# Norm columns transposed into the next group's accumulator, and x loaded by itself one block ahead

## The chip, the cores and the metric

The kernel runs on one core of one Trainium2 chip. The metric is device time in microseconds (us), the median of the runs. The kernel before took 2122.87 us (median of 3 runs, 2119.78 to 2123.72).

Five engines work side by side, each with its own queue in program order: PE (TensorE, matrix products and transposes), DVE (VectorE), ACT (ScalarE), POOL (GpSimd) and SP (SyncE, which here only issues DMA transfers; ACT can issue them too). An instruction that waits for another engine holds up all that is queued behind it on its own.

## The reference

One layer over two sequences, the prompt (s = 0, 1024 tokens) and the sample (s = 1, 2048 tokens), model width 1024. The input is modulated and projected; half of the width goes through a windowed attention, the other half through a differential attention with 4 heads of two softmaxes each; the results are gated, projected and normalised with the input.

```python
def diff_attention(...):          # per block of 128 queries, 4 heads, 2 maps
    logits = jnp.einsum('bqhmd,bkhmd->bhmqk', qb, kh) * (HEAD_DIM ** -0.5)
    p = jax.nn.softmax(logits + bias[None, :, None], axis=-1)
    w = p[:, :, 0] - lam * p[:, :, 1]
    o = jnp.einsum('bhqk,bkhe->bqhe', w, vh)
    ...
    o = rms_norm(o, subln_w) * (1.0 - lambda_init)

def hybrid_layer(x, c, ...):
    u = x * (1.0 + scale[:, None]) + shift[:, None]
    qa, ka, va, ga, qb, kb, vb, gb = jnp.split(u @ w_in, SPLIT_OFFSETS, axis=-1)
    oa = window_gqa(qa, ka, va, sink, rel_bias) * jax.nn.silu(ga)
    ob = diff_attention(qb, kb, vb, ...) * jax.nn.silu(gb)
    h = jnp.concatenate([oa, ob], axis=-1) @ w_out
    return layer_norm(ALPHA * x + gate[:, None] * h, ln_g, ln_b)
```

The part that the change touches is the factor of `rms_norm`, one number per query and head, and the loading of x for the last line.

## The kernel before

Up to about 1144 us the projections and the windowed attention run. Then comes the differential attention, unit by unit (128 queries of one head), 64 units of the sample sequence and after them 16 of the prompt. Two units of the sample, or one unit of the prompt holding two blocks, form a group of 256 queries. `slot(n, ...)` does unit n in four steps; in a step PE has, in this order, the logits of unit n (L826, into a tile `lg`), the values of earlier groups (L882 to L884, into the group's accumulator, the left half of the PSUM tile `ac` that the code calls `G["O"]`), and four transposes of a unit three slots back (L864, into a tile `tp`, of which there are two). DVE adds the bias and takes the minimum (L831), ACT takes the exponential (L839, 2048 wide for the sample, 1024 for the prompt), DVE and POOL combine the two maps (L841, L844, L848, L850), ACT and DVE split each transposed tile into a high and a low part (L866, L867; L867 is the last reader of `tp`).

When a group's values are done, ACT copies them out (`osb`, L887) and they are stored (L888; by SP, in the last slots by ACT). In the second step of a later slot `square_sum` follows: PE transposes `osb` into the right half of the same accumulator tile (L897, twice), ACT squares each of the two transposes in place and sums it (L899, twice), ACT and DVE form the argument (L901, L903), and POOL takes the power -1/2 (L909) into two columns of a tile `four`. Two groups fill its four columns, so there are 48 sums and 24 stores. `store` turns the four columns into rows: a transpose on PE (L915), a copy on ACT (L917), a DMA on SP (L918) into `frow`.

The order on PE is written out by hand through all slots. The order on the other engines is set by the compiler's scheduler up to unit 79; from slot 80 on (the transition, about 1807 to 1848 us) all engines follow the code, and `outputs()` is stepped in between: it loads and splits the output weights and begins with the output. `load_rest(t)` loads the parts of output block t, `gate_parts(t)` and `join(t)` (POOL and ACT, L1046 to L1057) combine them, `output` multiplies (L1081 to L1083), adds gate and x (L1086, L1087) and normalises; L1123 stores the block. There are 24 blocks of 128 tokens, `load_rest` runs three blocks ahead and `join` two.

Of the kernel before, what the change touches and what calls it, by code (L numbers as in the profile page):

```python
# [11 lines left out]
F32 = mybir.dt.float32  # L12
# [8 lines left out]
P = 128  # L21
# [46 lines left out]
def hybrid_layer(ctx, tc, x_prompt, x_sample, c_prompt, c_sample, w_in, w_out, w_ada, b_ada, ln_g, ln_b,  # L68
                 attn_sink, lambda_q1, lambda_k1, lambda_q2, lambda_k2, subln_w, rel_bias, oh, eye,
                 y_prompt, y_sample):  # L70
    nc = tc.nc
    xs = (x_prompt, x_sample)
# [14 lines left out]
    def tp():  # L87
        return ps_tp.tile([P, 512], F32, tag="tp", name="tp")
# [59 lines left out]
    def load_x(tb, d):  # L148
        s, t0 = (0, tb * CH) if tb < 2 else (1, (tb - 2) * CH)
        xt = x_p.tile([P, 4, P], F32, tag="x", name="x")  # L150
        nc.sync.dma_start(out=xt, in_=xs[s][t0:t0 + CH, d * P:(d + 1) * P].rearrange("(j p) d -> p j d", p=P))
        return xt
# [235 lines left out]
    def fill(n):  # L388
        for _ in range(n):
            next(steps, None)  # L390
# [110 lines left out]
    with tc.issue_after(wload[6]):  # L501
# [15 lines left out]
        for i in range(2):  # L517
            bg = sm2.tile([1, D], F32, tag="bg", name="bg")
            nc.sync.dma_start(out=bg, in_=b_ada[2 * D:3 * D].rearrange("(o d) -> o d", o=1))
            for q in range(2):  # L520
                cs = slice(q * 512, (q + 1) * 512)
# [218 lines left out]
    order = [(s, h) for s in (1, 0) for h in range(HB)]  # L740
# [45 lines left out]
    def prefetch(n, j):  # L786

        s, h, i, g = units[n]
        if j == 1:
            for u in units[n + 1:n + (3 if n >= EARLY - 1 else 2)]:  # L790
                if u[3] == asked[0] + 1 and (u[0] == 0 or u[3] == units[n + 1][3]):
                    load_queries(u[3])
        if n in staged and j == 2:
            stage(staged[n])
        if i == (4 if s else 2) and j == 2 and (s, h) != units[-1][:2]:
            load_head(*next_head[s, h])
        if n + 1 < N and units[n + 1][2] == 0 and j == 3:
            load_keys(*units[n + 1][:2], range(2, SEQS[units[n + 1][0]] // CH))
# [72 lines left out]
    def values(g, piece):  # L871
        s, h, i = groups_of[g]
        T = SEQS[s] // P
        G = groups_[g]
        Vt = heads[s, h][2]
        if piece == 0:
            G["O"] = ac()
        a = G["O"][:, :QG]
        for kb in range(piece * 2, piece * 2 + 2):
            kq, c = divmod(kb, 4)  # L880
            H, L = G["PT"][kq]
            nc.tensor.matmul(a, lhsT=Vt[kq][:, 0, c, :], rhs=H[:, c, :], start=(kb == 0), stop=False)  # L882
            nc.tensor.matmul(a, lhsT=Vt[kq][:, 0, c, :], rhs=L[:, c, :], start=False, stop=False)  # L883
            nc.tensor.matmul(a, lhsT=Vt[kq][:, 1, c, :], rhs=H[:, c, :], start=False, stop=(kb == T - 1))  # L884
        if piece == T // 2 - 1:
            osb = e_p.tile([P, QG], F32, tag="osb", name="osb")
            nc.scalar.copy(osb, a)  # L887
            (nc.sync if now[0] < N * 4 else nc.scalar).dma_start(out=OT[s][h][:, i * P:i * P + QG], in_=osb)  # L888
            G["osb"] = osb

    def square_sum(g):
        s, h, i = groups_of[g]
        G = groups_[g]
        ss = st_p.tile([P, 2], F32, tag="ss", name="ss")
        ot = [G["O"][:, QG + b * P:QG + (b + 1) * P] for b in range(2)]
        for b in range(2):
            nc.tensor.transpose(ot[b], G["osb"][:, b * P:(b + 1) * P], ident)  # L897
        for b in range(2):
            nc.scalar.activation(ot[b], ot[b], AF.Square, accum_out=ss[:, b:b + 1])  # L899
        f = st_p.tile([P, 4], F32, tag="f", name="f")  # L900
        nc.scalar.activation(f[:, 0:2], G["s0"], AF.Square, scale=EPS ** 0.5)  # L901
        for b in range(2):
            nc.vector.tensor_scalar(out=f[:, 2 + b:3 + b], in0=ss[:, b:b + 1], scalar1=1.0 / P,  # L903
                                    scalar2=f[:, b:b + 1], op0=ALU.mult, op1=ALU.add)
        c = i % 4
        if c == 0:
            four[0] = four_p.tile([P, 4], F32, name="four")
        F = four[0]
        nc.gpsimd.tensor_tensor(out=F[:, c:c + 2], in0=f[:, 2:4], in1=mhalf, op=ALU.pow)  # L909
        del groups_[g]  # L910

        def store():

            pf = tp()
            nc.tensor.transpose(pf[0:4, 0:P], F, ident)  # L915
            fr = f_p.tile([4, P], F32, name="fr")
            nc.scalar.copy(fr, pf[0:4, 0:P])  # L917
            nc.sync.dma_start(out=frow[s][h, (i - 2) * P:(i + 2) * P].rearrange("(b p) -> b p", p=P), in_=fr)  # L918

        if c:  # L920
            stores.append((now[0] + 6, store))

    now, stores, four = [0], [], [None]

    def slot(n, extra, other=None):
        for j in range(4):
            now[0] = n * 4 + j
            if extra:
                fill(extra)
            if n < N:  # L930
                logits(n, j)
                prefetch(n, j)
            for g, piece in values_at.get(n, ()):
                if piece % 4 == j:
                    values(g, piece)
            if 0 <= n - LAG < N:
                transpose(n - LAG, j)
            if j == 1 and n in sums_at:
                square_sum(sums_at[n])
            if stores and stores[0][0] <= now[0]:  # L940
                stores.pop(0)[1]()
            if other is not None:
                next(other, None)

# [56 lines left out]
    xts = Views(lambda: value() if len(xts.made) < 3 else part(), 6)  # L1001
# [28 lines left out]
    def load_rest(t):  # L1030

        s, i = order[t]
        cs = slice(i * P, (i + 1) * P)
        d = dat.next().rearrange("p (n i q) -> p n i q", n=4, i=4)
        nc.sync.dma_start(out=d[:, 1], in_=OT[s][:, :, cs].rearrange("k r t -> r k t"))
        nc.sync.dma_start(out=d[:, 2], in_=frow[s][:, cs].partition_broadcast(P))
        nc.sync.dma_start(out=d[:, 3], in_=GB[s][:, :, cs].rearrange("k r t -> r k t"))
        nc.sync.dma_start(out=d[:, 0], in_=OA[s][:, :, cs].rearrange("i r t -> r i t"))
        xt = xts.next().bitcast(F32)
        nc.sync.dma_start(out=xt, in_=xs[s][cs, :])  # L1040
        Bs[t] = dict(s=s, i=i, d=d, xt=xt)

    def gate_parts(t):

        d = Bs[t]["d"]
        nc.gpsimd.tensor_tensor(out=d[:, 1], in0=d[:, 1], in1=d[:, 2], op=ALU.mult)  # L1046
        nc.gpsimd.tensor_tensor(out=d[:, 1], in0=d[:, 1], in1=d[:, 3], op=ALU.mult)

    def join(t):

        B = Bs[t]
        d = B["d"]
        B["oH"], B["oL"] = [v.rearrange("p (k q) -> p k q", k=KC) for v in os_.next()]
        for half in range(2):
            hs = slice(half * 4, half * 4 + 4)
            nc.scalar.copy(B["oH"][:, hs, :], d[:, half])
            nc.gpsimd.tensor_tensor(out=B["oL"][:, hs, :], in0=d[:, half], in1=B["oH"][:, hs, :].bitcast(F32),  # L1057
                                    op=ALU.subtract)
# [66 lines left out]
    order = [(s, i) for s in (1, 0) for i in range(SEQS[s] // P)]  # L1125
    NB = len(order)
    Bs = {}

    def outputs():

        todo = {0: lambda: load_rest(0), 4: lambda: load_rest(1), 6: lambda: load_gate(1), 8: load_norm,
                5: lambda: gate_parts(0), 11: lambda: join(0), 14: lambda: load_rest(2)}
        halves = [(k, n) for k in range(4) for n in range(2)] + [(k, n) for n in range(2) for k in range(4, KC)]
        blocks = out_steps()
        for step in itertools.count():
            if step in todo:
                todo[step]()
            if halves:
                split_weights(*halves.pop(0))
            if step >= 12 and next(blocks, 0) == 0:  # L1140
                return
            yield

    def out_steps():
        for t in range(NB):
            if t == 8:
                load_gate(0)
            for j, _ in enumerate(output(Bs[t], t == NB - 1)):
                if j == 2 and t + 3 < NB:
                    load_rest(t + 3)  # L1150
                if j == 4 and t == 0:
                    gate_parts(1)
                    join(1)
                if j == 12 and t + 2 < NB:
                    gate_parts(t + 2)
                    join(t + 2)
                yield
            del Bs[t]
            yield
# [7 lines left out]
    with tc.manual_schedule(engines=ENGINES):  # L1167
        for n in range(N, max(sums_at) + 1):
            slot(n, 0, other)
        for _ in range(8):  # L1170
            next(other)
        for _, store in stores:
            store()
        for _ in other:
            pass
    st.close()
# [26 lines left out]
```

## Time and profile before

| | us |
|---|---|
| median of 3 runs | 2122.87 |
| profiled execution | 2118.73 |
| its span, first to last instruction | 2116.9 |
| PE busy | 2059.4 (97%) |
| POOL / DVE / ACT busy | 1151.1 / 1300.3 / 1045.9 |
| differential attention, sample | about 1144 to 1660 |
| the same, prompt | about 1660 to 1807 |
| transition | about 1807 to 1848 |
| output blocks | about 1848 to 2108.8 |

The span is the time between the first and the last instruction of one execution; 1.8 us of that execution lie outside it. A busy share is an average over stages, so the stages are read one by one. The trace names each instruction by its line in the code, the tile it writes and the tiles it reads.

### The profile page before, as it was taken

The page shows a single profiled execution, that of the slowest core. Times are in us where ns is not written, and L with a number is a line of the kernel's source. Part 1 is how long each engine was busy: PE and PEld are TensorE (multiplying, and loading weights), DVE is VectorE, ACT ScalarE, POOL GpSimd, SP SyncE. Part 2 cuts the span into 40 slices and gives each one's busy share as a digit, 9 for nine tenths or more (in the row PEclk, how much of TensorE's full clock was granted, in tenths as well). Part 3 has the DMA queues.
Part 4 walks back from the last instruction along what each step waited for, and adds up shares of the span by engine and source line. Part 5 has one row for each costly group of instructions (what it writes and reads, how often), then busy time and mean ns, then how long its engine had stood idle before and what let it go on. Part 6 is the DMA issues. An engine that isn't in the chain of part 4 may idle for free.

```text
span 2116.9 us, 32562 instructions
## 1 busy us (share of the span) xinstructions
PE 2059.4 (97%) x11621; PEld 1769.6 (84%) x11621; DVE 1300.3 (61%) x2536; ACT 1045.9 (49%) x2046; POOL 1151.1 (54%) x830
## 2 busy tenths in 40 slices
PE   7999999999999999999999999999999999799998
PEld 4777898888988888888897888888888899788887
DVE  5335124222225777777654998989898999655555
ACT  5211113111015767777623777777777899622221
POOL 3213213212124344334353888888888899677774
PEclk9999999999999999999999999999999999999999
DMA  9685735435538868778454122122131353557763
GB/s 273 181 292 156 188 120 174 132 122 135 155 115 226 205 167 216 207 194 212 131 164 145 46 83 79 44 91 71 58 102 38 92 169 106 166 146 203 199 196 103
DMA packets 327337, 312.44 MB, mean 148 GB/s; under 512 B 19126, under 2 KB 284086, under 8 KB 326792
## 3 DMA queue, kind: packets, MB, share of 16 engines
q1 hardware_dynamic: 326456, 309.72, 51.4%
q8 instruction: 92, 1.51, 0.3%
q10 hardware_dynamic: 720, 0.66, 0.1%
q14 instruction: 69, 0.57, 0.1%
HBM read 212.70 MB, written 97.60 MB: 147 GB/s over the span
## 4 chain that ended last, share of the span: by engine, by line
PE 87%; DMA 5%; DVE 4%; ACT 1%; POOL 1%; issue 1%; SPq 1%; ACTq 0%; DVEq 0%; POOLq 0%
PE lg L826 14%; PE pj L187 12%; PE pj L188 12%; PE pj L189 12%; PE tp L864 6%; PE po L1083 4%; PE po L1082 4%; PE po L1081 4%; PE ac L882 3%; PE ac L884 3%; PE ac L883 3%; PE lgA L608 3%; PE tp L644 3%; PE ac L636 2%; PE ac L635 1%; DVE l L831 1%
## 5 line engine op out<-in xcount | busy, mean ns | idle before, releaser
L187 PE MATMUL pj<-uH,wH 128*128 128x512 f32 x1040 | 418.0, 402 | 3.4 <-DVE gg L258 3.4
L189 PE MATMUL pj<-uH,wL 128*128 128x512 f32 x1040 | 406.8, 391 | 0.0
L218 POOL TENSOR_TENSOR wL<-wr,wH 128x1024 fp32r<-128x1024 f32 x74 | 181.8, 2459 | 413.5 <-DVE wH L216 373.2
L188 PE MATMUL pj<-uL,wH 128*128 128x512 f32 x1040 | 406.4, 391 | 0.0
L850 POOL TENSOR_TENSOR l<-l,l 128x1024 f32<-128x1024 f32 x160 | 382.8, 2415 | 1.2
L826 PE MATMUL lg<-kt,Q 128*128 128x512 f32 x1280 | 374.8, 414 | 2.1 <-DVE gg L258 1.4
L839 ACT ACTIVATE l<-l,nm 128x2048 f32<-128x2048 f32 (+1 forms) x192 | 330.9, 1724 | 15.8 <-DVE nm L831 15.8
L831 DVE CUSTOM_DVE_ANT_0 l<-lg,W 128x1024 f32<-128x1024 f32 x192 | 233.5, 1216 | 21.4 <-PE lg L826 21.3
L866 ACT CAST pth<-tp 128x512 fp32r<-128x512 f32 x320 | 186.6, 584 | 119.6 <-PE tp L864 111.5
L826 PEld LDWEIGHTS lg<-kt,Q 128*128 128x128 f32 x1280 | 217.1, 189 | 31.9 <-DVE nm L831 2.0
L848 POOL TENSOR_SCALAR l<-l,s 128x1024 f32<-128x1024 f32 x160 | 179.3, 1134 | 100.2 <-DVE s L844 57.3
L189 PEld LDWEIGHTS pj<-uH,wL 128*128 128x128 f32 x1040 | 195.1, 188 | 42.2
L187 PEld LDWEIGHTS pj<-uH,wH 128*128 128x128 f32 x1040 | 195.5, 188 | 36.9 <-DVE gg L258 4.3
L867 DVE TENSOR_TENSOR ptl<-tp,pth 128x512 fp32r<-128x512 f32 x320 | 210.7, 686 | 17.8 <-ACT pth L866 16.4
L188 PEld LDWEIGHTS pj<-uL,wH 128*128 128x128 f32 x1040 | 195.8, 188 | 30.6
L864 PE MATMUL tp<-ident,l 128*128 128x128 f32 x1280 | 192.0, 272 | 5.8 <-DVE ptl L867 5.8
L623 POOL TENSOR_SCALAR l<-l,rcA 128x384 f32<-128x384 f32 (+1 forms) x144 | 81.0, 581 | 191.0 <-DVE rcA L617 97.3
L882 PE MATMUL ac<-pth,vt 128*128 128x256 f32 x640 | 180.9, 283 | 0.0
L884 PE MATMUL ac<-pth,vt 128*128 128x256 f32 x640 | 180.0, 281 | 0.0
L883 PE MATMUL ac<-ptl,vt 128*128 128x256 f32 x640 | 179.1, 280 | 0.0
L831 DVE CUSTOM_DVE_ANT_0 l<-lg,W,nm 128x1024 f32<-128x1024 f32 x128 | 164.0, 1281 | 20.9 <-PE lg L826 15.7
L864 PEld LDWEIGHTS tp<-ident,l 128*128 128x128 f32 x1280 | 147.9, 140 | 8.2 <-DVE ptl L867 5.0
(210 smaller groups left out, 4025.9 us busy)
## 6 DMA issues: line engine op xcount, KB each, us to landing
wr<-in_w_in SPq DMA_DIRECT2D x39, 1024.0 KB, 5.7
KAt<-ka SPq DMA_DIRECT2D x40, 384.0 KB, 7.1
QAt<-qa SPq DMA_DIRECT2D x24, 512.0 KB, 4.8
kt<-kb SPq DMA_DIRECT2D x24, 512.0 KB, 5.2
Q<-qb SPq DMA_DIRECT2D x48, 256.0 KB, 3.3
Q<-qb SPq DMA_DIRECT2D x96, 128.0 KB, 3.1
vt<-vb SPq DMA_DIRECT2D x48, 256.0 KB, 4.6
wa<-in_w_ada SPq DMA_DIRECT2D x32, 256.0 KB, 6.0
```

Of the source, the lines that this page charges most:

```text
L187: nc.tensor.matmul(acc, lhsT=a(k), rhs=b(k), start=(k == 0), stop=False)
L188: nc.tensor.matmul(acc, lhsT=a(k), rhs=bl(k), start=False, stop=False)
L189: nc.tensor.matmul(acc, lhsT=al(k), rhs=b(k), start=False, stop=(k == KC - 1))
L826: nc.tensor.matmul(L[:, c * CH:(c + 1) * CH], lhsT=G["Q"][:, v, m, b * P:(b + 1) * P], rhs=Kt[kt0 + c][:, m, :], start=(v == 0), stop=(v = ...
L831: nc.vector.tensor_tensor_reduce(out=half, in0=L, in1=W[:, off:off + 1024], scale=1.0, scalar=nm[:, m, 0:1] if s and hf else 3e38, op0=ALU ...
L839: nc.scalar.activation(e, e, AF.Exp, bias=nm[:, m, hf:hf + 1], scale=-1.0, accum_out=sums)
L850: nc.gpsimd.tensor_tensor(out=row[:, cs], in0=row[:, cs], in1=rows[n][1][:, cs], op=ALU.add)
L864: nc.tensor.transpose(pt[:, c * P:(c + 1) * P], rows[n][0][:, (j * 4 + c) * P:(j * 4 + c + 1) * P], ident)
L867: nc.vector.tensor_tensor(out=L[:, :, qs], in0=p3, in1=H[:, :, qs].bitcast(F32), op=ALU.subtract)
L882: nc.tensor.matmul(a, lhsT=Vt[kq][:, 0, c, :], rhs=H[:, c, :], start=(kb == 0), stop=False)
L883: nc.tensor.matmul(a, lhsT=Vt[kq][:, 0, c, :], rhs=L[:, c, :], start=False, stop=False)
L884: nc.tensor.matmul(a, lhsT=Vt[kq][:, 1, c, :], rhs=H[:, c, :], start=False, stop=(kb == T - 1))
```

## The change

`store` no longer takes a `tp` tile of its own six steps after its group's sum. It is kept until the next group's `square_sum` and transposes `four` into that group's accumulator tile, rows 0 to 3 of its left half, whose values have been copied to `osb` by then. The last store of all still takes a `tp` tile. In the output part the load of x is taken out of `load_rest` into `load_x`: x of block 0 at step 10, x of block t+1 at the fourth step of block t; `load_rest(t + 3)` moves from the third step of a block to the seventh, and `load_rest(2)` from step 14 to step 16.

```diff
@@ -909,16 +909,18 @@
         nc.gpsimd.tensor_tensor(out=F[:, c:c + 2], in0=f[:, 2:4], in1=mhalf, op=ALU.pow)
         del groups_[g]
 
-        def store():
-
-            pf = tp()
+        if stores:
+            stores.pop()(G["O"])
+
+        def store(pf):
+
             nc.tensor.transpose(pf[0:4, 0:P], F, ident)
             fr = f_p.tile([4, P], F32, name="fr")
             nc.scalar.copy(fr, pf[0:4, 0:P])
             nc.sync.dma_start(out=frow[s][h, (i - 2) * P:(i + 2) * P].rearrange("(b p) -> b p", p=P), in_=fr)
 
         if c:
-            stores.append((now[0] + 6, store))
+            stores.append(store)
 
     now, stores, four = [0], [], [None]
 
@@ -937,8 +939,6 @@
                 transpose(n - LAG, j)
             if j == 1 and n in sums_at:
                 square_sum(sums_at[n])
-            if stores and stores[0][0] <= now[0]:
-                stores.pop(0)[1]()
             if other is not None:
                 next(other, None)
 
@@ -1036,9 +1036,12 @@
         nc.sync.dma_start(out=d[:, 2], in_=frow[s][:, cs].partition_broadcast(P))
         nc.sync.dma_start(out=d[:, 3], in_=GB[s][:, :, cs].rearrange("k r t -> r k t"))
         nc.sync.dma_start(out=d[:, 0], in_=OA[s][:, :, cs].rearrange("i r t -> r i t"))
-        xt = xts.next().bitcast(F32)
-        nc.sync.dma_start(out=xt, in_=xs[s][cs, :])
-        Bs[t] = dict(s=s, i=i, d=d, xt=xt)
+        Bs[t] = dict(s=s, i=i, d=d)
+
+    def load_x(t):
+        s, i = order[t]
+        xt = Bs[t]["xt"] = xts.next().bitcast(F32)
+        nc.sync.dma_start(out=xt, in_=xs[s][i * P:(i + 1) * P, :])
 
     def gate_parts(t):
 
@@ -1129,7 +1132,7 @@
     def outputs():
 
         todo = {0: lambda: load_rest(0), 4: lambda: load_rest(1), 6: lambda: load_gate(1), 8: load_norm,
-                5: lambda: gate_parts(0), 11: lambda: join(0), 14: lambda: load_rest(2)}
+                5: lambda: gate_parts(0), 11: lambda: join(0), 10: lambda: load_x(0), 16: lambda: load_rest(2)}
         halves = [(k, n) for k in range(4) for n in range(2)] + [(k, n) for n in range(2) for k in range(4, KC)]
         blocks = out_steps()
         for step in itertools.count():
@@ -1146,7 +1149,9 @@
             if t == 8:
                 load_gate(0)
             for j, _ in enumerate(output(Bs[t], t == NB - 1)):
-                if j == 2 and t + 3 < NB:
+                if j == 3 and t + 1 < NB:
+                    load_x(t + 1)
+                if j == 6 and t + 3 < NB:
                     load_rest(t + 3)
                 if j == 4 and t == 0:
                     gate_parts(1)
@@ -1169,8 +1174,7 @@
             slot(n, 0, other)
         for _ in range(8):
             next(other)
-        for _, store in stores:
-            store()
+        stores.pop()(tp())
         for _ in other:
             pass
     st.close()
```

In the changed kernel's line numbers L915, L917 and L918 are L917, L919 and L920, and the load of x is L1044 instead of L1040.

PE in the sample sequence, kernel before, at a step with a store (`four` holds the four norm columns):

```order
L884 MATMUL ac<-pth,vt 128x256
L864 MATMUL tp<-ident,l_13634 128x128 [waits DVE_49]
L864 MATMUL tp<-ident,l_13634 128x128 x3
L915 MATMUL tp<-ident,four 4x128 [waits DVE_49,PE_49,Pool_49]
L826 MATMUL lg<-kt,Q 128x512 x4
L882 MATMUL ac<-pth,vt 128x256 [waits Activation_49]
```

The transpose of the norm columns waits there for DVE and POOL. PE in the changed kernel, at a step with a store:

```order
L864 MATMUL tp<-ident,l_13725 128x128 [waits DVE_49]
L864 MATMUL tp<-ident,l_13725 128x128 x3
L897 MATMUL ac<-ident,osb 128x128 [waits Activation_49]
L897 MATMUL ac<-ident,osb 128x128
L917 MATMUL ac<-ident,four 4x128 [waits Activation_49,Pool_49]
L826 MATMUL lg<-kt,Q 128x512 [waits DVE_49]
L826 MATMUL lg<-kt,Q 128x512 x3
L882 MATMUL ac<-pth,vt 128x256
```

The transpose has moved directly behind the two transposes of the next group's sum, and waits for ACT and POOL. ACT in the sample sequence, kernel before, around a store and the next sum:

```order
L839 ACTIVATE l_13934,s0g<-l_13934,nm 128x2048 [waits DVE_49]
L917 COPY fr<-tp 4x128 [waits DMAHW0_49,PE_49]
L866 CAST pth<-tp 128x4x128 [waits PE_49] x2
L899 ACTIVATE ac,ss<-ac 128x128 [waits PE_49,Activation_49]
L839 ACTIVATE l_13989,s_13988<-l_13989,nm 128x2048 [waits DVE_49,Pool_49]
L899 ACTIVATE ac,ss<-ac 128x128 [waits Activation_49]
```

ACT in the changed kernel at the same place:

```order
L839 ACTIVATE l_13928,s0g<-l_13928,nm 128x2048 [waits DVE_49]
L866 CAST pth<-tp 128x4x128 [waits PE_49] x2
L899 ACTIVATE ac,ss<-ac 128x128 [waits PE_49,Activation_49]
L839 ACTIVATE l_13978,s_13977<-l_13978,nm 128x2048 [waits DVE_49,Pool_49]
L899 ACTIVATE ac,ss<-ac 128x128 [waits Activation_49]
L919 COPY fr<-ac 4x128 [waits DMAHW0_49,PE_49]
```

The copy of the rows has moved behind the second of the next sum's squares; an exponential stands between the two squares, as before. ACT in the transition, kernel before, at the fourth of its five stores of a group (`DMAHW0` to `DMAHW7` are eight semaphores that transfers take in turn; a transfer is issued when the one before it on its semaphore has landed):

```order
L1022 ACTIVATE wo<-kt,wsub 128x512
L887 COPY osb<-ac 128x256 [waits DMAHW1_49,PE_49]
L888 DMA ot_81<-osb 128x256 [waits DMAHW0_49,Activation_49]
L1022 ACTIVATE wo<-kt,wsub 128x512
L1056 CAST pth<-l_19029 128x512 [waits DMAHW6_49]
```

The same place in the changed kernel:

```order
L1022 ACTIVATE wo<-kt,wsub 128x512
L887 COPY osb<-ac 128x256 [waits PE_49]
L888 DMA ot_81<-osb 128x256 [waits DMAHW2_49,Activation_49]
L1022 ACTIVATE wo<-kt,wsub 128x512
L1059 CAST ptl<-l_19006 128x512 [waits DMAHW5_49]
```

The store has another semaphore, because one transfer more or fewer stands ahead of it in the order of issue.

## Rows read from the trace of the kernel before

**Rows 1.** The page's section on the chain that ended last, by engine and line.

```profile
PE 87%; DMA 5%; DVE 4%; ACT 1%; POOL 1%; issue 1%; SPq 1%; ACTq 0%; DVEq 0%; POOLq 0%
```

**Rows 2.** Three stages: length, busy us (instructions) by engine, clock, DMA share, GB/s.

```profile
1144.00:1660.00 516.00, 502.28 (x3371) 455.71 (x3372) 466.75 (x891) 396.57 (x660) 434.01 (x271) 1.00 0.25 76
1660.00:1807.00 147.00, 146.06 (x996) 133.72 (x995) 137.36 (x300) 132.41 (x288) 136.69 (x90) 1.00 0.43 128
1848.00:2108.80 260.80, 260.71 (x1151) 213.19 (x1149) 138.17 (x239) 57.81 (x97) 184.54 (x160) 0.99 0.62 174
```

**Rows 3.** Sixteen steps of the sample sequence, same columns.

```profile
1453.29:1488.14 34.85, 33.92 (x229) 30.93 (x230) 31.39 (x61) 26.77 (x46) 29.18 (x19) 1.00 0.13 39
```

**Rows 4.** PE's waits, 1000 to 1807 us: total us, times, longest.

```profile
PE tp L915 <- DVE ptl L867: 13.1, 14, 0.9
```

**Rows 5.** PE's instructions, a step without and one with a store: start, length.

```profile
1484.53 0.60 PE L864 MATMUL tp<-ident,l 128*128 128x128 f32 x4
1484.89 0.48 PE L826 MATMUL lg<-kt,Q 128*128 128x512 f32 x1
...
1486.62 0.60 PE L864 MATMUL tp<-ident,l 128*128 128x128 f32 x4
1488.14 0.27 PE L915 MATMUL tp<-ident,four 128*4 128x128 f32 x1 [0.93 <-DVE ptl L867]
1488.16 0.94 PE L826 MATMUL lg<-kt,Q 128*128 128x512 f32 x3
```

**Rows 6.** PE at a sum of squares, sample sequence.

```profile
1474.37 0.38 PE L897 MATMUL ac<-ident,osb 128*128 128x128 f32 x2
1474.51 0.94 PE L826 MATMUL lg<-kt,Q 128*128 128x512 f32 x3
```

**Rows 7.** ACT over the same sum.

```profile
1475.05 0.28 ACT L899 ACTIVATE ac<-ac 128x128 f32<-128x128 f32 x1
...
1475.34 2.00 ACT L839 ACTIVATE l<-l,nm 128x2048 f32<-128x2048 f32 x1
...
1477.32 0.27 ACT L899 ACTIVATE ac<-ac 128x128 f32<-128x128 f32 x1
1477.52 0.19 ACT L899 ACTIVATION_READ_ACCUMULATOR ac<-ac 128x1 f32 x1
```

**Rows 8.** PE and ACT at a sum of the prompt sequence.

```profile
1786.01 0.94 PE L826 MATMUL lg<-kt,Q 128*128 128x512 f32 x3
...
1786.84 1.15 ACT L839 ACTIVATE l<-l,nm 128x1024 f32<-128x1024 f32 x1
...
1788.17 0.19 ACT L899 ACTIVATION_READ_ACCUMULATOR ac<-ac 128x1 f32 x1
```

**Rows 9.** ACT and PE in the transition, waits in brackets.

```profile
1823.76 0.59 ACT L866 CAST pth<-tp 128x512 fp32r<-128x512 f32 x1 [4.00 <-DMA ot<-osb]
...
1844.53 0.72 ACT L1022 ACTIVATE wo<-kt,wsub 128x512 fp32r<-128x512 f32 x1 [7.61 <-DMA l<-gb]
...
1846.95 0.36 ACT L887 COPY osb<-ac 128x256 f32<-128x256 f32 x1
...
1825.12 0.66 PE L864 MATMUL tp<-ident,l 128*128 128x128 f32 x4 [2.84 <-DVE ptl L867]
...
1847.36 0.69 PE L897 MATMUL ac<-ident,osb 128*128 128x128 f32 x2 [3.51 <-ACT osb L887]
```

**Rows 10.** PE behind the last of these waits: busy, clock, as in rows 2.

```profile
1848.00:1850.00 2.00, 2.00 (x7) 1.52 (x6) 1.65 (x5) 1.35 (x7) 1.25 (x3) 0.50 0.96 180
1850.00:1852.00 2.00, 2.00 (x9) 1.66 (x8) 0.00 (x0) 0.00 (x0) 1.92 (x3) 0.82 0.85 311
```

**Rows 11.** SP and POOL in the output blocks: two issues, one wait.

```profile
1905.39 0.35 SPq L1123 DMA_DIRECT2D out<-pth  x1
...
1908.87 5.00 SPq L1040 DMA_DIRECT2D vt<-in_x_sample  x1
...
POOL l L1046 <- DMA l<-frow: 18.3, 11, 2.8
```

## The prediction, made before the changed kernel was run

> **What bounds the kernel now.** I read the chain that ended last first: 87% of it is PE [rows 1], so a microsecond counts where PE is held up. The stages then say where PE has time left: it is busy 502.28 of 516.00 us in the sample's differential attention, 146.06 of 147.00 in the prompt's, and 260.71 of 260.80 in the output blocks [rows 2]. Time can be won only in the gaps of the first and in the transition; it can be lost anywhere. Sixteen steps of the sample, with one store in them, take 34.85 us, of which PE works 33.92, DVE 31.39, POOL 29.18 and ACT 26.77 [rows 3]: PE sets the pace, the others have 3.5 to 8.1 us to spare, and the 0.93 us that PE misses is one wait. That wait is at the transpose of the norm columns, L915, for DVE's subtraction L867: 14 times between 1000 and 1807 us, 13.1 us in all [rows 4]. The store takes one of two `tp` tiles, and DVE has not yet read the one it gets.
>
> **What goes at the stores.** In a step without a store the logits L826 start 1484.89 - 1484.53 = 0.36 us behind the first of the four transposes L864; with one, 1488.16 - 1486.62 = 1.54 [rows 5]. The difference, 1.18 us, leaves that step: the 0.93 of wait and what the refilling of PE costs. 14 stores have it; the six other stores before the transition show no such wait and give back nothing I count.
>
> **What comes at the sums.** The transpose now stands directly behind the two L897 of the next group's sum and ahead of the next logits, and the rows of the order give it a wait for ACT and one for POOL. POOL's power is a whole group old by then, so it is free. ACT's is not. The L897 just ahead has already waited for ACT's copy `osb`; a further wait for ACT can only be for something ACT does later, and the only later ACT work on that accumulator tile is the two squares L899, which work in place on the half that the L897 have just written. The rows of ACT in the changed kernel fit: the copy of the new rows stands behind the second square.
>
> So PE would wait for the second square, and between the two squares ACT has an exponential. At 1474 us the first square starts at 1475.05, the exponential takes 2.00, and the reading of the second square's sum ends at 1477.52 + 0.19 = 1477.71 [rows 7]. PE starts 0.05 us after ACT is done where a row shows that pair: copy ended at 1846.95 + 0.36 = 1847.31, L897 at 1847.36 [rows 9]. L826 follows L915 by 0.02 [rows 5]. The logits would start at 1477.78 instead of 1474.51 [rows 6], 3.27 us late. Behind L917 in PE's queue stand the logits, the values and the next transposes, so nothing on PE fills this. DVE's L831 waits for the logits, and the exponentials for DVE; they have the 3.5 us and more of rows 3 to catch up, so I add nothing for them. Net of a sample store: 3.27 - 1.18 = +2.09; 14 of them **+29.3 us**.
>
> Six more stores meet sums while the exponentials are 1024 wide (1.15 us): there the second square is read at 1788.17 + 0.19 = 1788.36, L826 would be at 1788.43 instead of 1786.01, 2.42 us late [rows 8]; six of them **+14.5 us**. (24 stores: 14, these 6, 3 in the transition, and the last one in a `tp` tile as before.)
>
> Bounds of the wait: from below, no new wait at all (a rival, below); from above the same 3.27 and 2.42 with a fall of the clock behind each.
>
> [...]
>
> **The clock.** PE now idles from the end of L897 at 1474.37 + 0.38 = 1474.75 to about 1477.76, 3.0 us. [...] Behind the wait of 2.84 us at 1825.12, four L864 took 0.66 [rows 9], about the 0.60 of rows 5: no fall. 3.0 is nearer to 2.84, so I take 0; the upper end is 14 x 1.7 = 24 us. [...]
>
> **The transition.** ACT issues the stores of the last groups there and hangs twice for a semaphore that an earlier transfer holds: 4.00 and 7.61 us; PE's waits of 2.84 and 3.51 follow [rows 9]. In the changed order one transfer more or less stands ahead, so each store draws another semaphore. The one that hung behind the load of `gb` now follows a short store of the norm rows; its wait and the fall of the clock go, 3.51 + 1.7 = 5.2. Against it stand three new waits for the squares; they lie next to each other there, so each is about 1.0 (an estimate from two squares of 0.27 and 0.19 each in rows 7, with the way there and back), and two of them fall into waits that PE has anyway. I take **-4.1 us**; the ends are -8 (the 2.84 goes too) and +3 (the 3.51 stays, and all three come on top).
>
> **The output blocks.** Removing the x load from the parts and issuing it for itself changes no instruction on PE, DVE or POOL. x for the next block now goes out directly behind a block's store, the parts behind it instead of ahead. SP spends up to 5.00 us on one x load, and POOL already waits 11 times, 18.3 us, for a part (`frow`) [rows 11]. PE is at 100% and the parts are joined two blocks ahead, so I take 0. From below it is 0 as well, since PE has no gap to close. From above: parts 5.00 us later, of which POOL's free time, (260.80 - 184.54) / 24 = 3.2 per block, hides most; 1.8 us, once in two blocks of the 16 of the sample, is +14.
>
> **The sum.** 29.3 + 14.5 - 4.1 = +39.7 us. The profiled execution took 2118.73 (span 2116.9 and 1.8 outside), which gives 2158.4; it was 4.1 below the median of the runs shown, so on that base **2163 us**.
>
> **Rivals.**
> - *The wait isn't for the squares* (the other side: faster). If ACT's wait at L917 ends with the copy `osb`, PE goes straight on, the 13.1 us of rows 4 and the 5.2 of the transition go, and the time is about 2105. It decides where the logits start no more than 0.3 us behind L897. For it: the two halves of the tile don't overlap. Against it: the L897 ahead has that wait already.
> - *The clock falls at each sample wait*: +24, about 2187. For it: 3.51 did it. Against it: 2.84 did not.
> - *The parts come late*: output blocks longer than before, +14, about 2177. For it: POOL's 18.3 us for `frow`. Against it: the same bytes pass in the same time, and an x load stood between two blocks' parts before as well.
> - *The stores' gain is hidden*: DVE's subtraction is late for an L864 instead, and the wait comes back there. That would add at most 14 x 0.93 = 13, about 2176; the L864 of rows 5 wait for nothing, and the order has one tile less in use, so I give it little and count it with the parts.
>
> **Chances.** Forecast 0.64 (its own range 2155 to 2170, by the ends of the transition); clock 0.18; late parts or tiles 0.10; no wait for the squares 0.05; between it and the forecast, within 0.2%, 0.03. A difference of 0.2%, 4 us, is about what can be told from no change. The range 2150 to 2188 leaves out the fast rival and the clock together with late parts. Faster 0.05, same 0.03, slower 0.92.
>
> **What would show it.** In the profile after: a row "L917 waits for ACT's L899" with some 20 to 23 waits, the longest near 3, about 58 us in all (14 x 3.0, 6 x 2.2 and the transition); no wait of L915's kind for L867; the sixteen steps 34.85 + 2.1 = about 36.9 us long at a clock of 1.00 (below it: the clock rival); output blocks still at 11 us each with PE busy throughout; no wait of 3.5 us near 1847 + 43. The prediction is wrong if L826 starts within 0.3 us of L897 at these sums, or if the blocks grow.

## The result and the profile after

The changed kernel takes 2184.64 us (median of 5 runs, 2180.34 to 2188.64) against 2122.87 before (5 runs): 1.0293 of the time before, 95% interval 1.0273 to 1.0313. It is slower by some 62 us. The profiled execution took 2180.34 us, its span is 2178.3, 61.4 longer than before.

The waits of PE through the differential attention and the transition (total us, times, longest), kernel after; these rows stand where [rows 4] stood:

```profile
PE ac L917 <- ACT ac L899: 56.8, 20, 3.2
PE ac L917 <- ACT f L901: 3.7, 3, 1.6
PE po L1084 <- ACT Q L1059: 2.3, 1, 2.3
PE tp L864 <- DVE ptl L867: 1.9, 4, 0.7
```

Twenty waits of the store's transpose for a square, where before there were 14 for DVE's subtraction; these have gone without coming back at L864 (1.9 us). The second row is the three stores in the transition. It names L901, which ACT does right behind the squares, but there too L917 starts 0.14 us after the second square is read (1876.31 + 0.19 = 1876.50, L917 at 1876.64). The third row is the first product of the output, which waits there for its input. PE and ACT at one store of the sample (start, length, instruction, wait in brackets), which answer to [rows 5 to 7]:

```profile
1248.61 0.38 PE L897 MATMUL ac<-ident,osb 128*128 128x128 f32 x2
1252.09 0.27 PE L917 MATMUL ac<-ident,four 128*4 128x128 f32 x1 [3.09 <-ACT ac L899]
1252.11 0.70 PE L826 MATMUL lg<-kt,Q 128*128 128x512 f32 x2
```

```profile
1249.30 0.27 ACT L899 ACTIVATE ac<-ac 128x128 f32<-128x128 f32 x1
...
1249.58 1.99 ACT L839 ACTIVATE l<-l,nm 128x2048 f32<-128x2048 f32 x1
...
1251.57 0.26 ACT L899 ACTIVATE ac<-ac 128x128 f32<-128x128 f32 x1
1251.76 0.18 ACT L899 ACTIVATION_READ_ACCUMULATOR ac<-ac 128x1 f32 x1
1252.39 0.26 ACT L919 COPY fr<-ac 4x128 f32<-4x128 f32 x1 [0.45 <-PE ac L917]
```

The second square is read at 1251.76 + 0.18 = 1251.94, L917 starts 0.15 us later, and the logits 3.50 us behind L897 instead of 0.14. At a store of the prompt the exponential is shorter, and so is the wait:

```profile
1743.15 0.38 PE L897 MATMUL ac<-ident,osb 128*128 128x128 f32 x2
1745.77 0.37 PE L917 MATMUL ac<-ident,four 128*4 128x128 f32 x1 [2.24 <-ACT ac L899]
```

3.09 - 2.24 = 0.85 us, just what the exponentials differ by (2.00 and 1.15, [rows 7, 8]).

Four cycles of sixteen steps with one store each, kernel after, columns as in [rows 3] (the clock stands in front of the last two):

```profile
1215.10:1252.09 36.99, 33.90 (x230) 30.85 (x231) 31.58 (x61) 26.88 (x45) 29.14 (x19) 1.00 0.12 37
1252.09:1289.09 37.00, 33.91 (x230) 30.91 (x230) 31.56 (x61) 26.89 (x45) 27.57 (x19) 0.99 0.37 112
1364.29:1404.01 39.72, 36.63 (x229) 33.24 (x230) 31.66 (x61) 26.88 (x45) 29.09 (x19) 0.92 0.11 34
1517.90:1557.64 39.74, 36.65 (x230) 33.26 (x231) 31.66 (x61) 26.89 (x45) 29.05 (x19) 0.93 0.11 34
```

In the first two PE works 33.9 us as before and waits 3.09 instead of 0.93: 37.0 against 34.85. In the others the same matrix products take 36.6 us. The stretches of 2 us behind the store at 1364.29 show why:

```profile
1364.30:1366.30 2.00, 2.00 (x6) 1.63 (x7) 0.09 (x1) 0.26 (x1) 2.00 (x2) 0.50 0.05 9
1366.30:1368.30 2.00, 2.00 (x12) 2.00 (x10) 1.23 (x2) 0.00 (x0) 1.05 (x2) 0.50 0.00 0
1368.30:1370.30 2.00, 2.00 (x7) 1.61 (x7) 0.74 (x2) 0.59 (x1) 0.00 (x0) 0.51 0.00 0
1370.30:1372.30 2.00, 2.00 (x15) 1.83 (x15) 1.45 (x3) 0.82 (x2) 0.00 (x0) 1.00 0.41 124
```

PE idled 3.09 us, and for the next 6 its clock was granted at 0.50. Behind the equally long wait at 1252.09 it stayed at 1.00:

```profile
1252.10:1254.10 2.00, 2.00 (x14) 1.82 (x15) 0.87 (x2) 0.26 (x1) 2.00 (x2) 1.00 0.02 5
```

Set the first L897 of each sum side by side in the two traces, and the whole loss can be read off as steps of the difference:

```
stretch                         what                             us
sample, 14 stores               steps of +3.34 to +3.36          +46.9
                                further, at 8 of the 14          +13.6
sample, 14 steps of the store   -1.19 to -1.22 each              -16.9
prompt, 6 stores                steps of +2.39                   +14.3
                                further, at 5 of the 6            +7.9
transition and output blocks                                      -3.6
start (other work, ends earlier) and rounding                      -0.8
sum, as between the two spans                                    +61.4
```

The output blocks were as long as before and PE was busy throughout:

```profile
1930.00:2169.70 239.70, 239.70 (x1065) 196.39 (x1064) 127.44 (x218) 53.42 (x84) 169.32 (x145) 1.00 0.66 183
```

POOL's wait for `frow` shrank from 18.3 us [rows 11] to 6.1. From 1912 to 2168 us, kernel after:

```profile
POOL ve L1100 <- DMA l<-frow: 3.8, 2, 1.9
...
POOL l L1049 <- DMA l<-frow: 2.3, 6, 0.6
```

### The profile page after: what moved, and what is told of

It reads as the page before. It is cut to its first block, busy times and chain, and to the rows that moved or that the text cites. A ratio compares the mean times of both kernels' runs of the same rounds, so it can differ in the third digit from the quotient of the medians.

```text
span 2178.3 us, 32604 instructions
## 1 busy us (share of the span) xinstructions
PE 2079.4 (95%) x11621; PEld 1787.4 (82%) x11621; DVE 1306.9 (60%) x2536; ACT 1049.4 (48%) x2046; POOL 1152.4 (53%) x830
## 4 chain that ended last, share of the span: by engine, by line
PE 88%; DMA 4%; issue 2%; ACT 2%; DVE 2%; POOL 1%; SPq 1%; ACTq 0%; DVEq 0%; POOLq 0%
PE lg L826 14%; PE pj L187 12%; PE pj L188 12%; PE pj L189 11%; PE tp L864 6%; PE po L1086 4%; PE po L1085 4%; PE po L1084 4%; PE ac L882 3%; PE ac L884 3%; PE ac L883 3%; PE lgA L608 3%; PE tp L644 3%; PE ac L636 2%; PE ac L635 1%
## 5 line engine op out<-in xcount | busy, mean ns | idle before, releaser
L826 PE MATMUL lg<-kt,Q 128*128 128x512 f32 x1280 | 387.2, 425 | 2.1 <-DVE gg L258 1.4
L826 PEld LDWEIGHTS lg<-kt,Q 128*128 128x128 f32 x1280 | 224.1, 195 | 33.1 <-DVE nm L831 2.1
L864 PE MATMUL tp<-ident,l 128*128 128x128 f32 x1280 | 195.3, 276 | 1.9 <-DVE ptl L867 1.9
L882 PE MATMUL ac<-pth,vt 128*128 128x256 f32 x640 | 184.6, 288 | 0.0
L884 PE MATMUL ac<-pth,vt 128*128 128x256 f32 x640 | 183.1, 286 | 0.0
L831 DVE CUSTOM_DVE_ANT_0 l<-lg,W,nm 128x1024 f32<-128x1024 f32 x128 | 164.0, 1281 | 23.4 <-PE lg L826 16.6
L864 PEld LDWEIGHTS tp<-ident,l 128*128 128x128 f32 x1280 | 150.6, 142 | 4.1 <-PE lg L826 1.1
```

The lines of the kernel that those rows point to most:

```text
L826: nc.tensor.matmul(L[:, c * CH:(c + 1) * CH], lhsT=G["Q"][:, v, m, b * P:(b + 1) * P], rhs=Kt[kt0 + c][:, m, :], start=(v == 0), stop=(v = ...
L831: nc.vector.tensor_tensor_reduce(out=half, in0=L, in1=W[:, off:off + 1024], scale=1.0, scalar=nm[:, m, 0:1] if s and hf else 3e38, op0=ALU ...
L864: nc.tensor.transpose(pt[:, c * P:(c + 1) * P], rows[n][0][:, (j * 4 + c) * P:(j * 4 + c + 1) * P], ident)
```

## The experiments

Each run is timed beside the kernel before on its own chip, where that took 2117 to 2119 us instead of 2122.87; so what counts is the difference, not the absolute time that an expectation names.

The theory: the store's transpose waits until the second square is read, the exponential between the squares makes that wait long, PE has nothing else to do in it, and behind some of these waits its clock falls to 0.50. The loads are worth a few microseconds in the transition. Rivals: the loads carry a part of the loss; the transpose into an accumulator costs by itself, wherever it stands; the long cycles come from DVE and ACT running late.

**The loads alone.** The kernel before, with only the diff's second half (`load_x`, and `load_rest` at the seventh step).

> Only the loading of x and of the parts is changed as in the changed kernel; the stores of the norm columns stay as before. Theory (all of the loss is at the sums with a store): the sixteen steps of the sample stay at 34.85 us with one wait of 0.93 us each; the output blocks stay at 11.08 us; in the transition the wait of 3.5 us behind a store of ACT goes and with it the fall of the clock, so 3 to 5 us are won: 2118 to 2123 us. Rival (the parts come late): output blocks longer than before, up to +14 us, 2130 to 2137.

2113.29 us against 2118.10, 0.9973 (0.9962 to 0.9984). The loads win 4.8 us, as much as expected at most, and lose nothing: behind 1870 us PE waits nowhere. PE from 1790 to 1870 us:

```profile
PE tp L864 <- DVE ptl L867: 2.4, 5, 1.1
PE tp L915 <- DVE ptl L867: 1.2, 2, 0.9
PE po L1086 <- POOL Q L1060: 0.6, 1, 0.6
PE po L1084 <- ACT Q L1059: 0.2, 1, 0.2
```

No wait of 3.51 or 2.84 us is left of [rows 9]. The late parts are refuted.

**The store alone.** The kernel before, with only the diff's first part.

> Only the store into the next group's accumulator; x is loaded with the parts as before. Theory: the same 20 waits of L917 for the squares, 56 to 58 us in all, net of the 14 old waits +44, and 15 to 25 us for the clock behind them; the transition's gain of 3 to 4 us may be missing: 2184 to 2190 us. Rival (the loads carry a part of the loss): clearly below the changed kernel's 2184.6, 2175 or less.

2190.56 against 2118.10, 1.0345 (1.0322 to 1.0369): all of the loss, and the loads' gain missing. The difference, 72 us, is 5 more than the 61 to 67 expected. Its profile shows falls of the clock behind 10 of the 14 sample waits instead of 8, and two waits of 2.6 us in the transition. The twenty waits for the squares are the same to a tenth:

```profile
PE ac L917 <- ACT ac L899: 56.8, 20, 3.2
```

**One step later, two steps later.** The store's transpose is kept for one step after the sum, as shown here, or for two (`now[0] + 2`):

```diff
-            stores.pop()(G["O"])
+            due.append((now[0] + 1, stores.pop(), G["O"]))
...
             if j == 1 and n in sums_at:
                 square_sum(sums_at[n])
+            if due and due[0][0] <= now[0]:
+                _, store, pf = due.pop()
+                store(pf)
```

> As the changed kernel, but the store's transpose stands one step later on PE, behind the next logits, values and transposes. Theory (PE waits for the end of the second square, 3.34 us behind L897 in the sample, 2.48 in the prompt): of that wait some 2.1 us are now covered by the step, so L917 waits 1.1 to 1.2 us in the sample and 0.3 or less in the prompt; the clock stays at 1.00; against 1.2 us that the old wait cost in the step of its store the sample comes out even, and the transition gives 3 to 4: 2117 to 2123 us. Rival (the transpose into an accumulator costs by itself, wherever it stands): still above 2150.

> As the changed kernel, but the store's transpose stands two steps later on PE, 4.2 us behind L897, when both squares are done. Theory: L917 waits nowhere in the sample and in the prompt, the 14 old waits are gone (14 x 1.2 = 17 us), and the transition gives 3 to 4 us: 2101 to 2105 us, faster than before. Rival (some other thing than the squares makes it wait, or the wait for DVE's subtraction comes back at the next transposes): 2115 or more.

One step: 2115.03 against 2118.10, 0.9988 (0.9979 to 0.9998). Two steps: 2097.63 against 2118.10, 0.9910 (0.9895 to 0.9926). The wait one step later, and one of its stores:

```profile
PE ac L917 <- ACT ac L899: 15.3, 20, 1.1
```

```profile
1393.23 0.27 PE L917 MATMUL ac<-ident,four 128*4 128x128 f32 x1 [1.02 <-ACT ac L899]
```

The wait goes 3.09, 1.02, none as the transpose is moved by steps of some 2.1 us: what PE waits for is a point in time on ACT, not something in the transpose. Behind none of the 14 waits of 1.02 us did the clock leave 1.00. The kernel is 3 us faster than before, within the 0 to 6 expected. Two steps later a cycle is pure PE work:

```profile
1418.87:1452.63 33.76, 33.76 (x231) 30.97 (x229) 31.29 (x61) 26.66 (x45) 29.51 (x19) 1.00 0.29 87
```

That is the 34.85 of [rows 3] less 1.09, and 20 us faster than the kernel before, as expected (18 to 22). What remained on PE from 1144 to 1840 us is small; the price of the delay is the second row, where the next group's values must wait until the rows are copied out of their tile:

```profile
PE tp L864 <- DVE ptl L867: 2.7, 5, 1.0
PE ac L882 <- ACT fr L919: 2.2, 2, 1.4
```

**The wait filled.** The changed kernel, with products ahead of L917 whose result nobody reads:

```diff
+            busy()
             stores.pop()(G["O"])
...
+        L = ps_lg.tile([P, 1024], F32, name="lg")
+        for r in range(3 if s else 2):
+            for c in range(2):
+                for v in range(2):
+                    nc.tensor.matmul(L[:, c * CH:(c + 1) * CH], lhsT=Q[:, v, 0, b * P:(b + 1) * P],
+                                     rhs=Kt[kt0 + c][:, 0, :], start=(v == 0), stop=(v == 1))
```

> As the changed kernel, but ahead of the store's transpose PE multiplies a tile of logits (three times in the sample, twice in the prompt, 12 and 8 products of about 0.24 us) that nobody reads, so that most of the wait for the squares is filled with work. Theory (two parts: the wait holds PE up by 3.3 and 2.4 us, and the idling lowers the clock behind it, 21.5 us in the profile of the changed kernel): the logits start as late as in the changed kernel, the granted clock stays at 1.00 behind every store, 16 steps take 37.0 us each time, and the time is 20 to 23 us below the changed kernel's: about 2157 to 2165 on a base of 2118 to 2123. Rival (the cycles of 38 to 40 us come from something else than idling, such as DVE and ACT running late): they stay, and the time is 2175 or more.

2164.44 against 2117.11, 1.0219 (1.0202 to 1.0236): 47 us slower, where 39 to 42 was expected. That and the changed kernel had been measured on two chips, and the ratios left 15.7 us for the clock where the steps above give 21.5; so both ran once more on one.

> The changed kernel once more, beside the one with the wait filled, so that the share of the clock is a difference on one chip. Theory (21.5 us of the loss in the first profile stood behind waits at a lowered clock): 61 us above before, and 18 to 22 us above the kernel with the filled wait. Rival (the two earlier runs on two chips, 1.0293 and 1.0219 of before, give 15.7 us): 14 to 17 us above it, a part of the cycles over 37.0 us coming from the filling itself.

> The kernel whose wait PE fills with products that nobody reads, on the same chip as the changed kernel. Theory: 40 to 44 us above before (14 x 2.15, 6 x 2.4, less 3 in the transition), the clock 0.995 or more. Rival: 45 to 48 above before.

Changed kernel 2185.64 against 2118.83, 1.0310 (1.0296 to 1.0324); filled 2162.27, 1.0207 (1.0193 to 1.0220). The filled kernel is 43 us slower than before, within the 40 to 44 expected. The filling wins 23.4 us, or 21.8 by the two ratios: at the upper end of the 18 to 22 expected or a little above it, and not the 14 to 17 of the rival. The changed kernel itself is 67 us slower than before, 6 more than the 61 expected. Its cycles in this second execution, from the first to the fifth store of the sample:

```profile
1220.01:1257.00 36.99, 33.90 (x229) 30.85 (x230) 31.58 (x61) 26.88 (x45) 29.14 (x19) 0.99 0.12 37
1257.00:1296.67 39.67, 36.58 (x230) 33.16 (x231) 31.66 (x61) 26.87 (x45) 29.31 (x21) 0.93 0.34 105
1296.67:1335.24 38.57, 35.48 (x230) 32.26 (x230) 31.57 (x61) 26.88 (x45) 30.93 (x19) 0.95 0.25 76
1335.24:1373.42 38.18, 35.09 (x230) 31.89 (x231) 31.57 (x61) 26.87 (x45) 29.10 (x19) 0.97 0.11 35
```

Its second store waits 3.09 us as in the first execution, but there the clock stayed at 1.00 (37.00 us), and here it falls (39.67). In the second execution it falls behind 10 of the 14 sample waits and 3 of the 6 prompt ones, which by the steps above costs 19.3 + 4.9 = 24.2 us instead of 21.5; and its first sum comes 4.9 us later, behind work that the change does not touch. A cycle of the filled kernel:

```profile
1365.98:1402.99 37.01, 36.71 (x242) 33.06 (x243) 31.57 (x61) 26.87 (x45) 29.17 (x19) 1.00 0.11 37
```

As long as the changed kernel's short cycles, with 2.8 us more PE work in it and the clock at 1.00; the logits start as late as before (the L897 of the sums step by +3.35 and +2.40). All of its sample cycles but one are like this; that one, 38.2, has 0.9 us of waiting for a load of keys. So the loss has two parts that come apart: the wait, and the slow clock behind PE's idling (on the one chip the mean clock of the profiled execution is 0.984 with the idling and 0.998 with the wait filled).

**One step earlier.** The store's transpose ahead of the two L897 instead of behind them (`if j == 0 and n in sums_at and stores: ...` in `slot`, and nothing in `square_sum`).

> As the changed kernel, but the store's transpose stands one step earlier on PE, ahead of the two L897 of the sum instead of behind them. Theory: it then waits only for the copy of the values, which ended 1.5 us and more before that place, and the squares wait for it, not it for them: no wait of more than 0.1 us at it, a cycle of 33.8 us, 2096 to 2101 us. Rival (it holds up the L897 behind it, which must now wait until ACT has copied the rows out of the same tile): a wait of 0.5 to 1 us at L897 in each of the 20 sums, 2108 to 2115.

2102.57 against 2117.11, 0.9934 (0.9911 to 0.9957): 15 us won, 2 to 7 less than expected (2096 to 2101 is 17 to 22 below a base of 2118). Its cycle is the expected one:

```profile
1446.66:1480.41 33.75, 33.75 (x231) 30.94 (x229) 31.30 (x61) 26.66 (x46) 29.20 (x18) 1.00 0.12 40
```

L897 waits nowhere for the copy, so the rival fell. One store of the prompt waits 0.7 us for POOL's power, where no wait above 0.1 was expected. What is missing against the two-step kernel lies mostly in the transition, where the sums drift from 1.4 to 4.7 us behind that kernel's; the first product of the output waits there 2.5 us for its input, and the clock falls behind it (a mean of 0.97 from 1790 to 1850 us).

**Two steps later, x loaded as before.** 

> The store two steps later as in the fourth run, but x loaded with the parts as before. Theory (the loads are worth what the transition gives, by the semaphore that ACT's store draws): the 14 old waits are gone, 17 us, and the wait of about 3.5 us in the transition with its fall of the clock is back: 2100 to 2104 us, 3 to 5 above the kernel that has both. Rival (the store alone does it all): the same as the kernel that has both, within 2 us.

2105.93 against 2117.11, 0.9943 (0.9923 to 0.9963); the kernel with both was at 0.9910, so by the ratios the loads are worth 7 us here (9 by the medians; the two kernels ran on different chips), more than the 3 to 5 expected. Waits of the size of [rows 9] are back, with a fall of the clock behind each (a mean of 0.94 from 1790 to 1850 us); PE from 1800 to 1840 us:

```profile
PE ac L917 <- ACT f L901: 3.4, 1, 3.4
PE tp L864 <- DVE ptl L867: 3.0, 2, 2.6
```

So the loads remove both, as they did alone, and I had counted on one.

## Why the prediction was right, and where it was not

- *The wait for the squares.* Right, in place, cause and size. +3.27 us at a sample store was +3.35; the 0.08 is the way from ACT to PE, 0.15 at L917 where I took the 0.05 of another pair. +2.42 in the prompt was +2.39. The number of waits, 20, and their sum, "about 58 us" with the transition, were 20 and 56.8 + 3.7.
- *The step of the store.* -1.18 was -1.19 to -1.22. Together the net terms +29.3 and +14.5 were +30.0 and +14.3.
- *The transition.* -4.1 was -3.6, but by luck: of two waits there the loads remove both (last experiment), and three new waits for squares (1.55, 1.23 and 0.95 us, where I let one of about 1.0 stand) and the 2.34 us ahead of the output's first product, with a fall of the clock behind it (0.50 from 1895.9 to 1899.3 us), take much of that back.
- *The clock.* This step failed: "3.0 is nearer to 2.84, so I take 0" was +21.5 us, as counted by the steps above (24.2 in the second execution); filling the wait won 23.4 on one chip. I treated the length of the idling as what decides, with one row on each side, 3.51 and 2.84 us [rows 9]. The runs do not bear that out: of 14 waits of 3.09 us, 8 were followed by a fall, and of the prompt's six of 2.24 us, shorter than both, five were. The rival held in part only: the clock did not fall "at each sample wait", and it fell in the prompt too. Its price, 14 x 1.7 = 24 for the sample alone, came out near the 21.5 by luck: 13.6 in the sample and 7.9 in the prompt. The 1.7 for one fall, here and in the 5.2 of the transition, is 2 us at a clock of 0.50 and 2 at 0.82, 1.36 us lost [rows 10], and the 0.31 by which two L897 took longer just ahead, 0.69 instead of 0.38 [rows 9, 6]; after the change a fall cost 1.2 to 2.8.
- *The output blocks.* 0 was right, and the mechanism of the late parts had the wrong sign: issued behind x, the parts are waited for less, not more (POOL waits 6.1 us for `frow`; with the loads as before, in the run with the store alone, 21.3).
- *Time.* 2163 + 21.5 = 2184.5, against 2184.64. The range held the result only because it reached up to the clock rival; the forecast's own range, 2155 to 2170, did not.

Of the two halves of the accumulator tile the trace shows that PE's write to the left one waited 3.09 us for ACT's square in the right one; that the wait is needed is not shown, since no run leaves it out.

What stays open: why the clock falls behind one wait of 3.09 us and not behind the next. Length and place of the wait do not decide it alone, since the same store goes both ways in two executions of the same kernel. What the rows do show is an order: in both executions the sample's cycles come as 37.0, 39.7, 38.6 and 38.2 us, over and over, from the fourth store on in the first (four cycles from 1327.28 to 1480.84, and the next four) and from the first store on in the second. No run here was made to tell what sets it.

## What to carry to other kernels

A scratch place that is free by address may still be in use by its tile: here PE waited 3.09 us to write to the left half while ACT worked in the right one. Before borrowing half of a tile, read on the other engine's queue what works on the rest of it and what stands between, since the wait here was for all of that (squares of 0.27 and 0.26 us, an exponential of 1.99 between them). Where the borrowed place stands decided: behind the readers, or ahead of them, it cost nothing here (33.76 and 33.75 us a cycle), between them 3.1 us and a clock of 0.50 behind 8 of the 14 waits. And price a wait of two or three microseconds on PE in a tight loop with the clock behind it, 1.2 to 2.8 us for a fall here, even if one such wait elsewhere went by without, as the 2.84 us of the kernel before did.

## What was not expected of the hardware

In the changed kernel, idling of PE of 2.24 us was followed by a fall of the granted clock to 0.50 in five of six cases, and 3.09 us in eight of fourteen (three of six and ten of fourteen in its second execution). 2.84 us in the kernel before was followed by none, 2.61 us in the last experiment by one, and fourteen idlings of 1.02 us by none. Two short ones close together were: in the run one step later PE idled 1.22 and then 0.62 us at 1834 us in the transition, and the clock stood at 0.50 from 1835.3 to 1838.6. A fall lasted 3.4 or 6.8 us in the changed kernel's trace and cost 1.2 to 2.8 us of PE's time.
